# Memory keys turned by transposing DMAs in 16-bit halves, joined where a head's attention begins

## The chip, the cores and the metric

The kernel runs on one core of one Trainium2 chip. The metric is the device time of one execution in microseconds. The kernel is compared with itself after one change; the inputs and the result are the same.

## The reference

One decoder layer over 256 tokens of width 2048, in fp32: half a SwiGLU block, a mixer of two head groups, cross-attention over 256 memory rows, half a SwiGLU block, and a final norm. The change touches only the keys of the cross-attention:

```python
def cross_attention(hn, memn, w_q, w_kv, w_o):
    q = (hn @ w_q).reshape(b, s, X_HEADS, X_HEAD_DIM)      # 4 heads of 512
    kv = memn @ w_kv
    k = kv[..., :D_MODEL].reshape(b, m, X_HEADS, X_HEAD_DIM)
    v = kv[..., D_MODEL:].reshape(b, m, X_HEADS, X_HEAD_DIM)
    scores = jnp.einsum('bshd,bmhd->bhsm', q, k) * (X_HEAD_DIM ** -0.5)
    probs = jax.nn.softmax(scores, axis=-1)
    out = jnp.einsum('bhsm,bmhd->bshd', probs, v).reshape(b, s, D_MODEL)
    return out @ w_o
```

A score sums over the 512 features of a head, so queries and keys must both lie with features on the partitions, while the projection leaves them with tokens (or memory rows) on the partitions. Somebody has to turn them.

## The kernel before

Every fp32 operand of a large product is split into two parts, hi (a cast on ACT, line 147) and lo (a subtraction on DVE, line 148), and a product is three matmuls: hi by hi, lo by hi, hi by lo. All large matmuls are issued in line 411; their tiles are named after the unit (mk0, mk1, wo, xq, xo) with P, Q or R behind. A unit multiplies eight chunks of 256 input features by two blocks of 512 output columns for both token blocks of 128. Some chunks ("S" in the lists of kinds) use seven block products in place of eight, with sums of the weight blocks formed on DVE (tiles ending in t, lines 320 to 324). Weights come by one 1 MB load a chunk from SP's queue (lines 318 and 341) into three raw buffers, and are split into two pairs of buffers.

The order of TensorE's instructions is that of the program, pinned by hand. The other engines' orders, SP's DMA issues among them, are made by a list scheduler that goes by the program's order and by when operands and buffers are ready in its model; on the chip each engine then runs its own list in order. While a chunk is multiplied, `side_step` runs after every six matmuls and takes one piece of other work from the list `side`: generators that yield the number of steps to wait. `later` holds functions that are called after a number of chunks (0: with the chunk whose end put them there). Buffers come from rotating pools: `s2` (six of 128x512 fp32), `m4` (twelve of 128x1024), and four PSUM banks for everything that isn't an accumulator (`bank`).

The units stand in this order: mk0 and mk1 (keys of heads 0 and 1, then 2 and 3), wo (two halves of the mixer's output), xq (queries of heads 0 and 1, then 2 and 3), xo (two halves). A key unit leaves, for each head, two tiles of 128 memory rows by 512 features (`kr`, tile name mk). Before the change `memory_keys` turns them in two pieces of side work a head: four TensorE transposes (line 1248) into a PSUM bank, and one DVE copy (line 1249) into the m4 tile mkT. At the head's attention, `attend_memory` first turns and splits the queries (xqTp, xqT, line 1286), then splits the whole of mkT with one cast and one subtraction of 1024 columns (`split4`, tile mkh, which names both parts), waits four steps of side work, and multiplies queries by keys (xs, line 152).

The feed-forward blocks already turn their activations by DMA (`rows_done` and `joined`, lines 657 to 679). ACT separates the two 16-bit halves of each fp32 word (f1w), a transposing DMA on SP turns both halves of 128 columns at a time (f1a), and ACT interleaves the halves again when the tile is needed (f1r).

Of the kernel before, what the change touches and what calls it, by code (L numbers as in the profile page):

```python
# [10 lines left out]
U16 = mybir.dt.uint16  # L11
# [4 lines left out]
P = 128  # L16
T = 256
TB = 2
# [15 lines left out]
def layer_kernel(  # L34
# [22 lines left out]
    nc = tc.nc  # L57
# [13 lines left out]
    def nm(s):  # L71
        uid[0] += 1
        return f"{s}_{uid[0]}"

    def m4(s):
        return mid.tile([P, 1024], F32, tag="m4", name=nm(s))

    def s2(s):
        return tmp.tile([P, 512], F32, tag="s2", name=nm(s))

    def bank(s):
        return trp.tile([P, 512], F32, tag="tr", name=nm(s))
# [18 lines left out]
    ident = const.tile([P, P], F32, name="ident")  # L101
# [17 lines left out]
    h = const.tile([P, TB, D], F32, name="h")  # L119
# [26 lines left out]
    def split(hi, lo, src):  # L146
        nc.scalar.copy(hi, src)  # L147
        nc.vector.tensor_tensor(lo, src, hi.bitcast(F32), ALU.subtract)  # L148

    def products(o, passes):  # L150
        for i, (a, b) in enumerate(passes):
            nc.tensor.matmul(o, a, b, start=i == 0, stop=i == len(passes) - 1)
# [70 lines left out]
    def laid(kind, k, tb):  # L223
        return BASE[kind].index(f"A{tb + 1}{k + 1}")
# [199 lines left out]
    def side_add(gen):  # L424
        side.append([now[0], gen])

    def side_run(item):
        try:
            item[0] = now[0] + next(item[1])
        except StopIteration:  # L430
            side.remove(item)
# [16 lines left out]
    def until(done):  # L448

        while not done():  # L450
            side_run(side[0])

    def have(pairs, i):
        until(lambda: pairs[i] is not None)
        return pairs[i]
# [3 lines left out]
    later = []  # L459
# [192 lines left out]
    def ffn(s, get, rs, wgu, wd, on_block, first=None, on_token_block=None):  # L652
        acts = [None] * 22
        pairs = [None] * 22

        def rows_done(c, rows_):
            turned_ = m4(s + "a").bitcast(U16).rearrange("p (b c t) -> p b c t", b=TB, c=8)

            def turned(tb):
                w = s2(s + "w").bitcast(U16)  # L660
                nc.scalar.copy(
                    w.rearrange("p (h c) -> p h c", h=2),
                    rows_[tb].bitcast(U16).rearrange("p (c h) -> p h c", h=2),
                )
                nc.sync.dma_start_transpose(turned_[:, tb], w)
                for q in range(2):
                    acts[2 * c + q] = turned_

            for tb in range(TB):
                later.append((tb, lambda tb=tb: turned(tb)))  # L670

        def joined(i):
            turned_ = have(acts, i).rearrange("p b (h c) t -> p b c t h", h=2)
            raw = s2(s + "r")
            words = raw.bitcast(U16).rearrange("p (i t h) -> p i t h", i=4, h=2)
            q = 2 * (i % 2)
            for tb in range(TB):
                j, k = laid(KINDS_D[i], 0, tb), laid(KINDS_D[i], 1, tb)
                nc.scalar.copy(words[:, j:k + 1:k - j], turned_[:, tb, q:q + 2])
            return raw.rearrange("p (i t) -> p i t", i=4)  # L680
# [12 lines left out]
        def inner(i):  # L693
            if pairs[i] is None:
                raw = joined(i)
                pairs[i] = Pair(s + "a", KINDS_D[i])
                fill(s + "a", pairs[i], raw)
# [59 lines left out]
        for n, idx in enumerate(turns):  # L757
            half = n % 2
# [468 lines left out]
    def m4r(s):  # L1227
        return mid.tile([P, 1024], F32R, tag="m4", name=nm(s))

    def split4(s, src):  # L1230

        hi, lo = m4r(s), m4r(s)
        split(hi, lo, src)
        return hi, lo

    mk = [None] * 4

    def memory_keys(hd, rows_):

        flat = m4("mkT")  # L1240
        dst = flat.rearrange("p (k t) -> p k t", k=4)
        for half in range(2):
            yield 2 if half else 4
            pv = bank("mkTp").rearrange("p (k t) -> p k t", k=2)
            for i in range(2):
                for tb in range(TB):
                    c = (2 * half + i) * P
                    nc.tensor.transpose(pv[:, i, tb * P:(tb + 1) * P], rows_[tb][:, c:c + P], ident)
            nc.vector.tensor_copy(dst[:, 2 * half:2 * half + 2, :], pv)
        mk[hd] = flat  # L1250

    def key_rows(cb):
        kr = [[s2("mk") for _ in range(TB)] for _ in range(2)]

        def late(ps=None):
            if ps is not None:
                for name, tb, j in BLOCKS:
                    nc.scalar.copy(kr[j][tb], ps[tb, j])
            for j in range(2):
                side_add(memory_keys(2 * cb + j, kr[j]))  # L1260

        return kr, late

    for cb in range(2):
        kr, late_mk = key_rows(cb)
# [12 lines left out]
    def attend_memory(hd, rows_):  # L1278
        qh, ql = [m4r("xqT").rearrange("p (k t) -> p k t", k=4) for _ in range(2)]
        for half in range(2):  # L1280
            yield 1 if half == 0 else 1
            pv = bank("xqTp").rearrange("p (k t) -> p k t", k=2)
            for i in range(2):
                for tb in range(TB):
                    c = (2 * half + i) * P
                    nc.tensor.transpose(pv[:, i, tb * P:(tb + 1) * P], rows_[tb][:, c:c + P], ident)
            split(qh[:, 2 * half:2 * half + 2, :], ql[:, 2 * half:2 * half + 2, :], pv)
        until(lambda: mk[hd] is not None)
        kh, kl = [t.rearrange("p (k m) -> p k m", k=4) for t in split4("mkh", mk[hd])]
        yield 4  # L1290
        ps = bank("xs")
        pv = ps.rearrange("p (b m) -> p b m", b=2)
        for tb in range(TB):
            passes = [(q[:, k, tb * P:(tb + 1) * P], m[:, k, :])
                      for k in range(4) for q, m in ((qh, kh), (qh, kl), (ql, kh))]
            products(pv[:, tb, :], passes)
        mx = tiny.tile([P, TB], F32, tag="xmx", name=nm("xmx"))
        nc.vector.tensor_reduce(out=mx, in_=pv, axis=AX.X, op=ALU.max)
        nc.vector.tensor_scalar_mul(mx, mx, -XS)
        pr = s2("pr").rearrange("p (b m) -> p b m", b=2)  # L1300
        den = tiny.tile([P, TB], F32, tag="xden", name=nm("xden"))
        for tb in range(TB):
            nc.scalar.activation(
                pr[:, tb, :], pv[:, tb, :], AF.Exp, bias=mx[:, tb:tb + 1], scale=XS,
                accum_out=den[:, tb:tb + 1],
            )
        nc.vector.reciprocal(den, den)
        for tb in range(TB):
            nc.vector.tensor_scalar_mul(pr[:, tb, :], pr[:, tb, :], den[:, tb:tb + 1])
        vh, vl = [t.rearrange("p (b c) -> p b c", b=2) for t in split4("mvh", mv[hd])]  # L1310
        yield 5
        ptv = bank("xpT").rearrange("p (b t) -> p b t", b=2)
        for b in range(2):
            for tb in range(TB):
                nc.tensor.transpose(
                    ptv[:, b, tb * P:(tb + 1) * P], pr[:, tb, b * P:(b + 1) * P], ident
                )
        ph, pl = [
            tmp.tile([P, 512], F32R, tag="s2", name=nm("xpTs")).rearrange("p (b t) -> p b t", b=2)
            for _ in range(2)  # L1320
        ]
        split(ph, pl, ptv)
        yield 3
        for half in range(2):
            pv = bank("xo").rearrange("p (k t) -> p k t", k=2)
            for i in range(2):
                dt_ = 2 * half + i
                passes = [(m[:, b, dt_ * P:(dt_ + 1) * P], p[:, b, :])
                          for b in range(2) for m, p in ((vh, ph), (vh, pl), (vl, ph))]
                products(pv[:, i, :], passes)  # L1330
            i = 2 * hd + half
            kind = KINDS_O[i]
            p = Pair("xo", kind)
            if kind == "N":
                split(p.base[0].rearrange("p k t -> p (k t)"),
                      p.base[1].rearrange("p k t -> p (k t)"),
                      pv.rearrange("p k t -> p (k t)"))
            else:
                raw = s2("xor").rearrange("p (k t) -> p k t", k=4)
                for k in range(2):  # L1340
                    for tb in range(TB):
                        nc.scalar.copy(raw[:, laid(kind, k, tb), :], pv[:, k, tb * P:(tb + 1) * P])
                fill("xo", p, raw)
            xo[i] = p
            yield 1
# [147 lines left out]
```

## Time and profile before

| | us |
|---|---|
| median of three runs | 2039.45 |
| lowest and highest | 2039.23 and 2040.15 |
| the profiled execution | 2038.53 |
| its span | 2036.8 |

| engine | busy us |
|---|---|
| TensorE (PE) | 2019.8 |
| weight loads (PEld) | 1671.6 |
| DVE | 1858.2 |
| ACT | 1297.9 |
| POOL | 36.3 |

The rows of the profile name an engine, a line, an operation and the tiles, written as out<-in. The span is what the profile covers; the time beside it is the execution's own. A matmul's busy time overlaps with that of its neighbours, since the engine takes the next before the last has ended, so its cost in a full queue is read from the distance of starts. In brackets behind a row stand the idle time of the engine before it and what ended that.

### The profile page before, as it was taken

Reading aid. Unit: us, or ns where it says so; the run is one execution under the profiler, and the core shown is the slowest. Engines: PE = TensorE matmul, PEld = TensorE weight load, DVE = VectorE, ACT = ScalarE, POOL = GpSimd, SP = SyncE. Lnnn points to the kernel's source line nnn. Section 1 sums busy time; section 2 is a strip of 40 time slices with the busy share of each in tenths; the row PEclk is TensorE's granted clock in tenths of the full one; section 3 lists DMA queues with packets and bytes.
Section 4 is the critical chain, followed back from the end, with each engine's and each line's share of the span. In section 5 each row is a group of like instructions: output and inputs, shape, how many; then the busy total and the mean of one; then the engine's idle time right before and its main releaser. Section 6 shows DMA issues by size and latency. Waiting matters only on the chain.

```text
span 2036.8 us, 24300 instructions
## 1 busy us (share of the span) xinstructions
PE 2019.8 (99%) x9235; PEld 1671.6 (82%) x9235; DVE 1858.2 (91%) x1998; ACT 1297.9 (64%) x1432; POOL 36.3 (2%) x57
## 2 busy tenths in 40 slices
PE   9999999999999999999999999999999999999998
PEld 8788888888888888888888888888888888888886
DVE  6999999999999978988988987899999999999998
ACT  7865656567665766655556655675656666676664
POOL 0000000000000010100000000000000000000000
PEclk9999999999999999999999999999999999999999
DMA  8666666666555565545555544556566656665563
GB/s 312 195 209 232 214 219 197 232 217 218 204 192 205 187 243 176 196 166 183 193 182 179 198 161 145 186 186 218 199 234 210 217 213 225 220 215 209 186 225 127
DMA packets 106884, 413.72 MB, mean 203 GB/s; under 512 B 53376, under 2 KB 55440, under 8 KB 59664
## 3 DMA queue, kind: packets, MB, share of 16 engines
q1 hardware_dynamic: 104320, 405.04, 57.5%
q0 software_dynamic: 2016, 6.30, 0.9%
q8 instruction: 72, 1.18, 0.2%
q10 hardware_dynamic: 432, 0.84, 0.1%
q14 instruction: 44, 0.36, 0.1%
HBM read 398.52 MB, written 2.10 MB: 197 GB/s over the span
## 4 chain that ended last, share of the span: by engine, by line
PE 85%; DVE 8%; issue 3%; ACT 1%; DMA 1%; SPq 0%; POOL 0%; POOLq 0%; DVEq 0%; ACTq 0%
PE f2gQ L411 13%; PE f1gQ L411 12%; PE f2dQ L411 6%; PE f1dQ L411 6%; PE f1gP L411 5%; PE f2gP L411 4%; PE xqQ L411 3%; PE f2dP L411 3%; PE f1dP L411 3%; PE woQ L411 2%; PE xoQ L411 2%; PE f2dR L411 2%; PE f1dR L411 2%; DVE f1gwl L148 2%; PE vQ L411 2%
## 5 line engine op out<-in xcount | busy, mean ns | idle before, releaser
L148 DVE TENSOR_TENSOR f1gwl<-f1gw,f1gwh 128x1536 fp32r<-128x1536 f32 (+2 forms) x94 | 181.6, 1934 | 23.3 <-ACT f1gwh L147 22.4
L147 ACT CAST f2gwh<-f2gw 128x1536 fp32r<-128x1536 f32 (+1 forms) x88 | 150.3, 1711 | 59.6 <-PE f2gQ L411 39.2
L148 DVE TENSOR_TENSOR f2gwl<-f2gw,f2gwh 128x1536 fp32r<-128x1536 f32 (+1 forms) x88 | 179.2, 2037 | 9.6 <-ACT f2gwh L147 9.6
L147 ACT CAST f1gwh<-f1gw 128x1536 fp32r<-128x1536 f32 (+2 forms) x94 | 153.0, 1629 | 44.4 <-PE f1gQ L411 18.0
L147 ACT CAST f1gth<-f1gt 128x1024 fp32r<-128x1024 f32 x76 | 79.9, 1051 | 102.7 <-DVE f1gt L320 67.7
L147 ACT CAST f2gth<-f2gt 128x1024 fp32r<-128x1024 f32 x82 | 85.9, 1049 | 69.7 <-DVE f2gt L324 40.4
L411 PE MATMUL f2gQ<-f2gwh,n4fh 128*128 128x512 f32 x317 | 124.2, 392 | 1.5 <-DVE f2gv L570 1.5
L411 PE MATMUL f2gQ<-f2gwh,n4fl 128*128 128x512 f32 x317 | 123.4, 389 | 0.0
L411 PE MATMUL f1gQ<-f1gwh,n1fl 128*128 128x512 f32 x286 | 111.4, 390 | 1.7 <-DVE n1fl L148 1.7
L411 PE MATMUL f1gQ<-f1gwh,n1fh 128*128 128x512 f32 x286 | 111.6, 390 | 0.0
L147 ACT CAST f2dwh<-f2dw 128x2048 fp32r<-128x2048 f32 (+1 forms) x44 | 77.4, 1759 | 47.5 <-PE f2dQ L411 39.5
L147 ACT CAST f1dwh<-f1dw 128x2048 fp32r<-128x2048 f32 (+1 forms) x44 | 77.3, 1757 | 43.7 <-PE f1dQ L411 42.7
L148 DVE TENSOR_TENSOR f1dwl<-f1dw,f1dwh 128x2048 fp32r<-128x2048 f32 (+1 forms) x44 | 92.0, 2091 | 11.3 <-ACT f1dwh L147 11.2
L148 DVE TENSOR_TENSOR f2dwl<-f2dw,f2dwh 128x2048 fp32r<-128x2048 f32 (+1 forms) x44 | 92.1, 2092 | 11.2 <-ACT f2dwh L147 11.1
L148 DVE TENSOR_TENSOR f2gtl<-f2gt,f2gth 128x1024 fp32r<-128x1024 f32 x82 | 99.7, 1219 | 1.0
L411 PE MATMUL f2gQ<-f2gwl,n4fh 128*128 128x512 f32 x317 | 96.7, 389 | 0.0
L148 DVE TENSOR_TENSOR f1gtl<-f1gt,f1gth 128x1024 fp32r<-128x1024 f32 x76 | 92.2, 1217 | 0.5
L411 PE MATMUL f1gQ<-f1gwl,n1fh 128*128 128x512 f32 x286 | 86.9, 389 | 0.0
L411 PEld LDWEIGHTS f2gQ<-f2gwh,n4fh 128*128 128x128 f32 x317 | 59.5, 188 | 15.9 <-DVE f2gv L570 3.7
L411 PEld LDWEIGHTS f2gQ<-f2gwl,n4fh 128*128 128x128 f32 x317 | 59.4, 188 | 12.3
L411 PEld LDWEIGHTS f2gQ<-f2gwh,n4fl 128*128 128x128 f32 x317 | 59.5, 188 | 12.1
L411 PE MATMUL f2gP<-f2gwh,n4fh 128*128 128x512 f32 x176 | 68.6, 390 | 0.0
(823 smaller groups left out, 6057.8 us busy)
## 6 DMA issues: line engine op xcount, KB each, us to landing
f2gw<-in_w_gu SPq DMA_DIRECT2D x88, 1024.0 KB, 5.1
f1gw<-in_w_gu SPq DMA_DIRECT2D x86, 1024.0 KB, 4.9
f1dw<-in_w_down SPq DMA_DIRECT2D x44, 1024.0 KB, 4.8
f2dw<-in_w_down SPq DMA_DIRECT2D x44, 1024.0 KB, 4.8
wow<-in_w_out SPq DMA_DIRECT2D x16, 1024.0 KB, 4.8
xqw<-in_w_xq SPq DMA_DIRECT2D x16, 1024.0 KB, 4.8
xow<-in_w_xo SPq DMA_DIRECT2D x16, 1024.0 KB, 4.8
qw<-in_w_in SPq DMA_DIRECT2D x8, 1024.0 KB, 4.8
```

What stands on the lines that cost most here:

```text
L147: nc.scalar.copy(hi, src)
L148: nc.vector.tensor_tensor(lo, src, hi.bitcast(F32), ALU.subtract)
L411: nc.tensor.matmul(self.banks[name], x, y, start=name not in self.begun, stop=self.left[name] == 0)
```

## The change

The two pieces of side work that turned the keys of a head are gone, with their transposes, banks and copies. In their place stands, called through `later`, the helper `turned_rows`, taken out of the feed-forward block: for each head and block of memory rows one ACT copy into an s2 tile (mkw) and one transposing DMA from SP's queue. The first head of a unit is turned with the chunk that ends the unit, the second one chunk later. `mk[hd]` now holds the turned halves. `keys_split`, called where `split4` was, joins them: for each half of the features two ACT copies into an s2 tile (mkr), then a cast and a subtraction of 512 columns into mkh and mkl. The feed-forward block calls the same helpers with its work unchanged.

```diff
+    def turned_rows(s, dst, src):
+        w = s2(s + "w").bitcast(U16)
+        nc.scalar.copy(
+            w.rearrange("p (h c) -> p h c", h=2), src.bitcast(U16).rearrange("p (c h) -> p h c", h=2)
+        )
+        nc.sync.dma_start_transpose(dst, w)
+
+    def tile_turned(s):
+        return m4(s).bitcast(U16).rearrange("p (b c t) -> p b c t", b=TB, c=8)
+
+    def by_block(turned):
+        return turned.rearrange("p b (h c) t -> p b c t h", h=2)
+
+    def words_of(raw, n):
+        return raw.bitcast(U16).rearrange("p (i t h) -> p i t h", i=n, h=2)
...
     def memory_keys(hd, rows_):
-        flat = m4("mkT")
-        dst = flat.rearrange("p (k t) -> p k t", k=4)
+        mk[hd] = tile_turned("mkT")
+        for tb in range(TB):
+            turned_rows("mk", mk[hd][:, tb], rows_[tb])
+
+    def keys_split(hd):
+        hi, lo = m4r("mkh"), m4r("mkl")
+        turned_ = by_block(mk[hd])
         for half in range(2):
-            yield 2 if half else 4
-            pv = bank("mkTp").rearrange("p (k t) -> p k t", k=2)
-            for i in range(2):
-                for tb in range(TB):
-                    c = (2 * half + i) * P
-                    nc.tensor.transpose(pv[:, i, tb * P:(tb + 1) * P], rows_[tb][:, c:c + P], ident)
-            nc.vector.tensor_copy(dst[:, 2 * half:2 * half + 2, :], pv)
-        mk[hd] = flat
+            raw = s2("mkr")
+            for tb in range(TB):
+                nc.scalar.copy(
+                    words_of(raw, 4)[:, tb::2], turned_[:, tb, 2 * half:2 * half + 2]
+                )
+            cols = slice(half * 512, (half + 1) * 512)
+            split(hi[:, cols], lo[:, cols], raw)
+        return hi, lo
...
             for j in range(2):
-                side_add(memory_keys(2 * cb + j, kr[j]))
+                later.append((j, lambda j=j: memory_keys(2 * cb + j, kr[j])))
...
-        until(lambda: mk[hd] is not None)
-        kh, kl = [t.rearrange("p (k m) -> p k m", k=4) for t in split4("mkh", mk[hd])]
+        kh, kl = [t.rearrange("p (k m) -> p k m", k=4) for t in keys_split(hd)]
```

More of the change, by code (lines that the diff above doesn't have):

```diff
@@ L656, in rows_done @@
         def rows_done(c, rows_):
-            turned_ = m4(s + "a").bitcast(U16).rearrange("p (b c t) -> p b c t", b=TB, c=8)
+            t = tile_turned(s + "a")
             def turned(tb):
[L660 to L665, printed above, removed]
+                turned_rows(s, t[:, tb], rows_[tb])
                 for q in range(2):
-                    acts[2 * c + q] = turned_
+                    acts[2 * c + q] = t
             for tb in range(TB):
@@ L672, in joined @@
         def joined(i):
-            turned_ = have(acts, i).rearrange("p b (h c) t -> p b c t h", h=2)
+            turned_ = by_block(have(acts, i))
             raw = s2(s + "r")
-            words = raw.bitcast(U16).rearrange("p (i t h) -> p i t h", i=4, h=2)
+            words = words_of(raw, 4)
             q = 2 * (i % 2)
```

## The prediction

> **What bounds the kernel now.** I read the engine totals first, then the stretches around the change, then the rows of the tiles it touches.
>
> ```profile
> PE 2019.8 (99%) x9235; PEld 1671.6 (82%) x9235; DVE 1858.2 (91%) x1998; ACT 1297.9 (64%) x1432; POOL 36.3 (2%) x57
> ```
>
> ```profile
> 1000.00:1020.00 20.00, 20.00 (x98) 16.55 (x97) 19.71 (x21) 11.78 (x11) 0.00 (x0) 1.00 0.52 187
> 1040.00:1060.00 20.00, 20.00 (x100) 16.52 (x99) 15.76 (x19) 7.71 (x7) 0.00 (x0) 1.00 0.51 180
> 1180.00:1200.00 20.00, 19.64 (x106) 16.53 (x105) 16.97 (x19) 14.72 (x16) 0.00 (x0) 1.00 0.46 159
> ```
>
> The first fence is the engines' totals, the second three stretches of 20 us, whose columns are length, then PE, weight load, DVE, ACT and POOL busy, granted clock, DMA share and GB/s. The keys are produced in the first two stretches and used from the third on. TensorE is full in all of them at a clock of 1.00, but for 0.36 us in the third; ACT has 5 to 12 us of every 20 free, DVE 0.3 to 4. So an instruction taken from TensorE is worth what it takes of its queue, as long as nothing new arrives late.
>
> That worth is not the duration that the tile's rows show.
>
> ```profile
> L1248 PE MATMUL mkTp<-ident,mk x32: 270/272/273, 1008.7 to 1071.3; 128*128 128x128 f32 x32
> L1249 DVE COPY mkT<-mkTp x8: 678/682/693, 1009.3 to 1071.7; 128x512 f32<-128x512 f32 x8
> ```
>
> ```profile
> 1008.25 0.39 PE L411 MATMUL mk1Q<-mk1wh,mTfh 128*128 128x512 f32 x1
> 1008.47 0.39 PE L411 MATMUL mk1Q<-mk1wh,mTfl 128*128 128x512 f32 x1
> 1008.70 0.60 PE L1248 MATMUL mkTp<-ident,mk 128*128 128x128 f32 x4
> 1009.06 0.48 PE L411 MATMUL mk1Q<-mk1wh,mTfh 128*128 128x512 f32 x1
> 1009.37 0.39 PE L411 MATMUL mk1Q<-mk1wh,mTfl 128*128 128x512 f32 x1
> ```
>
> Instructions overlap on this engine: two neighbouring matmuls of 512 columns start 0.22 to 0.23 us apart (1008.25, 1008.47), though each lasts 0.39. From the last start before the four transposes (1008.47) to the second after them (1009.37) 0.90 us pass, where two regular steps take 0.45. A group of four costs 0.45 us, 0.11 each.
>
> **The change, step by step.**
>
> *Removed from TensorE and DVE.* Four heads by two halves by four transposes are 32 transposes in 8 groups: 8 x 0.45 = 3.6 us, on a queue that is full at each of them, so this goes off the end. The 8 copies out of PSUM (8 x 0.682 = 5.5 us of DVE) go too. I give them nothing: TensorE waited for none of them. The eight banks and eight pieces of side work go as well; the pieces behind them in the side list (those of ya and yb) come up to a step earlier, which on a full TensorE is an exchange of order.
>
> *Added: turning.* For each head and token block one ACT copy that separates the 16-bit halves, and one transposing DMA on SP. The same pair stands in the first feed-forward block.
>
> ```profile
> L661 ACT COPY f1w<-f1gp x10: 1029/1036/1047, 101.8 to 472.9; 128x1024 uint16<-128x1024 uint16 x10
> L665 SPq DMA_TRANSPOSE f1a<-f1w x22: 1237/1275/1687, 52.0 to 478.1; - x22
> ...
> DMA to landing us min/median/max: 3.0/3.2/5.7
> ```
>
> The last line is the time from issue to landing. So 8 x 1.04 = 8.3 us of ACT and 8 x 1.28 = 10.2 us of SP's queue, landing after 3.2 us. The rows are complete at 1003.4 and 1048.1, and the keys are first read at 1188.
>
> ```profile
> L572 DVE TENSOR_TENSOR mk<-mk0Q,mk0z x1: 681/681/681, 1002.7 to 1002.7; 128x512 f32<-128x512 f32 x1
> L572 DVE TENSOR_TENSOR mk<-mk1Q,mk1z x1: 680/680/680, 1047.4 to 1047.4; 128x512 f32<-128x512 f32 x1
> L147 ACT CAST mkh<-mkT x4: 1047/1048/1054, 1188.2 to 1249.9; 128x1024 fp32r<-128x1024 f32 x4
> L148 DVE TENSOR_TENSOR mkh<-mkT,mkh x4: 1215/1217/1226, 1189.6 to 1251.0; 128x1024 fp32r<-128x1024 f32 x4
> ```
>
> The cover of the turning is some 140 us long, so its latency costs nothing. What it can cost is a place in ACT's and SP's order. ACT has room at the end of a key unit (6.25 us before 1001.87):
>
> ```profile
> 1001.87 1.92 ACT L147 CAST mk1wh<-mk1w 128x2048 fp32r<-128x2048 f32 x1 [6.25 <-PE mk0Q L411]
> 1012.14 1.91 ACT L147 CAST mk1wh<-mk1w 128x2048 fp32r<-128x2048 f32 x1 [0.50 <-PE mk1Q L411]
> 1006.23 0.33 SPq L318 DMA_DIRECT2D mk1w<-in_w_xkv  x1
> ```
>
> ```profile
> 1019.60 0.93 PE mk1P L411 x4
> ```
>
> ```profile
> mk1w<-in_w_xkv SPq DMA_DIRECT2D x8, 1024.0 KB, 4.9
> ```
>
> On SP a transpose waits at the head for its copy, and the weight load behind it waits too. The load of 1006.23 has 1 MB and lands after 4.9 us by its group's row, so at 1011.1; its cast began at 1012.14 and ended at 1014.05, and TensorE takes that weight at 1019.60. The load may slip 1.0 + 5.5 = 6.5 us before TensorE waits. Two transposes in a row hold SP 2.6 us. POOL's queue gets nothing. Cost: 0, with an end at what a longer hold gives (rival below).
>
> *Moved: joining and splitting.* One cast and one subtraction of 1024 columns become, per head, four joining copies, two casts and two subtractions of 512.
>
> ```profile
> L679 ACT COPY f1r<-f1a x44: 665/679/695, 433.3 to 629.1; 128x512 uint16<-128x512 uint16 x44
> L147 ACT CAST f1afh<-f1r x22: 611/616/632, 437.6 to 631.2; 128x512 fp32r<-128x512 f32 x22
> L148 DVE TENSOR_TENSOR f1afl<-f1r,f1afh x22: 678/682/686, 438.7 to 633.7; 128x512 fp32r<-128x512 f32 x22
> ```
>
> That is ACT 4 x 0.68 + 2 x 0.62 - 1.05 = +2.9 us a head and DVE 2 x 0.68 - 1.22 = +0.15. They are in the way only if the products of queries and keys come to TensorE's head before the split is done:
>
> ```profile
> 1189.57 1.22 DVE L148 TENSOR_TENSOR mkh<-mkT,mkh 128x1024 fp32r<-128x1024 f32 x1
> 1193.96 3.02 PE L152 MATMUL xs<-mkh,xqT 128*128 128x256 f32 x24
> 1196.90 1.05 ACT L147 CAST mkh<-mkT 128x1024 fp32r<-128x1024 f32 x1 [1.72 <-PE xs L152]
> 1198.11 1.22 DVE L148 TENSOR_TENSOR mkh<-mkT,mkh 128x1024 fp32r<-128x1024 f32 x1
> 1200.92 3.04 PE L152 MATMUL xs<-mkh,xqT 128*128 128x256 f32 x24
> 1244.53 1.22 DVE L148 TENSOR_TENSOR mkh<-mkT,mkh 128x1024 fp32r<-128x1024 f32 x1
> 1250.62 3.02 PE L152 MATMUL xs<-mkh,xqT 128*128 128x256 f32 x24
> ```
>
> Head 0: the split ends at 1190.79, the products begin at 1193.96, so 3.2 us are spare against 2.9 + 0.15 = 3.1 wanted; besides, the second half of the keys is wanted some 0.7 us after the products begin. Head 1: 1199.33 against 1200.92, 1.6 spare. But here ACT waited 1.72 us for a buffer that the products of head 0 set free (a cast needs one of the twelve m4 buffers); the joining copies need only s2 buffers and keys that have lain there for over 100 us, so they can run in that wait, and then 1.2 us of the 2.9 are left. Head 2: 1245.75 against 1250.62, 4.9 spare. Four joins and two casts can also be cut by a weight cast of 1.91. Ends: 0 and, for head 0, 1.9 us, for head 1 the uncovered 2.9 + 0.15 - 1.6 = 1.5, together 3.4. I take 0, as three of the four numbers (3.2, 4.9, and 1.6 + 1.72 of wait) cover it.
>
> A bound below nothing: the one stall of this stretch, TensorE waiting for the last query row.
>
> ```profile
> 1185.33 0.33 PE L1286 MATMUL xqTp<-ident,xqz 128*128 128x128 f32 x1 [0.36 <-ACT xqz L1351]
> ```
>
> ACT's order there is made anew with the joins in it, so 0.4 may go, or grow by a join or two (0.6 each). Taken: no change. The same holds for the second feed-forward block, whose order is also made anew and which is not full everywhere; the waits of its commonest matmul sum to 1.5 us, so I allow 1 us either way.
>
> ```profile
> L411 PE MATMUL f2gQ<-f2gwh,n4fh 128*128 128x512 f32 x317 | 124.2, 392 | 1.5 <-DVE f2gv L570 1.5
> ```
>
> *Sum.* -3.6 + 0 + 0 + 0. The profiled execution took 2038.53 us around a span of 2036.8, which becomes 2034.9; it lies 0.9 below the median of the runs, 2039.45, which becomes 2035.9. That is -0.18%, just inside 0.2% (4.1 us), about what a measurement of this kernel can tell from no change.
>
> **Rivals.**
>
> *More than the sum:* the 3.6 us and one or two of the small stalls with them, 4.1 to 6 us, so 2033.5 to 2035.3. For it: DVE is relieved by 5.5 + 4 x 1.22 - 8 x 0.68 = 4.9 us in a stretch where it was busy 19.71 of 20, and it ends the waits in the second feed-forward block. Against it: in the stretches of the change TensorE waited once, for ACT.
>
> *Each transpose is worth its duration:* 32 x 0.272 = 8.7 us, so 2030.7. For it: the row of the tile. Against it: the starts at 1008.47 and 1009.37. The Trainium skill ("TensorE: Matmul & The Clock Gate", Part 4) gives about 275 ns for a transpose in a kernel; by that figure the gain would be an estimated 8.8 us. The trace agrees with it as a duration (272 ns) and not as a cost in a full queue (0.11 us).
>
> *The heads wait for their keys:* part or all of 3.4 us is given back, so 2036.5 to 2039.3. For it: 3.1 wanted of 3.2 spare at head 0, and ACT busy 14.72 of 20 there before 5.8 us more come. Against it: the wait of 1.72 at head 1 and the idle ACT ahead of the query rows, in which joins can run.
>
> *Slower: SP's queue.* If a transpose is put on SP ahead of a load long before its copy can run, the load slips. It decides from 6.5 us of slip on. A hold as long as the longest wait that SP shows in this stretch, 9.6 us, costs 9.6 - 6.5 = 3.1 us of TensorE; there are four such places (two heads after each of two units), so up to 12.4 - 3.6 = +8.8 us, 2048.3, and with two of them 2042.0.
>
> ```profile
> SPq L341 <- DVE xqwl L148: 61.4, 10, 9.6
> ```
>
> ```profile
> 102.81 2.62 SPq L665 DMA_TRANSPOSE f1a<-f1w  x2
> 105.52 0.53 SPq L318 DMA_DIRECT2D f1gw<-in_w_gu  x1
> ```
>
> Against it: in the feed-forward block two transposes and the load behind them run through in 2.7 us. The Trainium skill ("VectorE: DVE Perf Modes", Rules for kernel authors) advises TensorE for a 128x128 transpose whenever PSUM will do as the target, which speaks against this change. [...]
>
> **How the numbers follow.** The forecast, 2035.4 to 2036.5: 0.41. More than the sum: 0.26. Durations: 0.05. Heads wait: 0.15. SP's queue: 0.13, of which 0.03 within 0.2%. Faster by over 0.2% takes the second and third, 0.31; within 0.2% the forecast, the heads and 0.03, 0.59; slower 0.10. The range 2033.5 to 2039.5 holds the forecast, the stalls both ways and the heads, 0.82; the likeliest case alone has 2035.4 to 2036.5.
>
> **What would show it.** Right: no mkTp rows; 32 fewer TensorE instructions, and the first product of the head 0 scores some 3.6 us earlier; TensorE at 20.00 in the stretches above; transposes of mk landing within some 6 us, and weight casts not waiting for loads longer than before. Wrong: idle time on TensorE or its weight load ahead of the scores (xs), released by ACT or DVE for mkh; an idle wait before wowh or mk1wh products; a weight load that starts late behind a transpose; or a head 0 that starts 8 us earlier.

## The result, and the profile after

The changed kernel takes 2033.45 us (median of eight runs, 2032.99 to 2035.32) against 2039.34 (eight runs, 2037.55 to 2040.94): ratio 0.9975, interval 0.9965 to 0.9984, so 5.9 us less by the medians. The profiled execution took 2033.63 us with a span of 2031.9, 4.9 less than the span before.

The engines' totals on the page of the changed kernel, then the stretches shown of the kernel before (the same columns):

```profile
PE 2015.5 (99%) x9203; PEld 1668.8 (82%) x9203; DVE 1853.6 (91%) x1994; ACT 1313.2 (65%) x1460; POOL 34.4 (2%) x57
```

```profile
1000.00:1020.00 20.00, 20.00 (x94) 16.54 (x93) 17.46 (x20) 14.81 (x15) 0.00 (x0) 1.00 0.78 215
1040.00:1060.00 20.00, 20.00 (x93) 16.54 (x92) 14.64 (x16) 11.29 (x11) 0.00 (x0) 1.00 0.78 204
1180.00:1200.00 20.00, 19.99 (x118) 17.20 (x117) 18.10 (x20) 17.50 (x26) 0.00 (x0) 1.00 0.31 109
```

32 matmuls fewer, DVE 4.6 us less, ACT 15.3 more, and TensorE still full, now in the third stretch too. The rows of the new work, by tile:

```profile
L153 ACT COPY mkw<-mk x8: 1037/1042/1046, 1004.5 to 1053.2; 128x1024 uint16<-128x1024 uint16 x8
L156 SPq DMA_TRANSPOSE mkT<-mkw x8: 1237/1316/4127, 1005.5 to 1054.2; - x8
DMA to landing us min/median/max: 3.2/5.3/6.6
```

```profile
L1263 ACT COPY mkr<-mkT x16: 658/684/712, 1173.7 to 1248.7; 128x512 uint16<-128x512 uint16 x16
L147 ACT CAST mkh<-mkr x8: 616/622/632, 1184.9 to 1251.1; 128x512 fp32r<-128x512 f32 x8
L148 DVE TENSOR_TENSOR mkl<-mkr,mkh x8: 680/684/693, 1186.1 to 1251.7; 128x512 fp32r<-128x512 f32 x8
```

To see where the time went, I cut the span twice: at the first mk0Q matmul of the key unit mk0 (2.2 us behind the unit's first matmul, in both kernels), and at the last matmul ahead of a wait that both kernels have in xo (for n4r). Of the timelines of TensorE, first the kernel before, then the changed one:

```profile
961.65 0.48 PE L411 MATMUL mk0Q<-mk0wh,mTfh 128*128 128x512 f32 x1
1317.46 0.39 PE L411 MATMUL xoQ<-xoth,xofl 128*128 128x512 f32 x1
```

```profile
962.43 0.48 PE L428 MATMUL mk0Q<-mk0wh,mTfh 128*128 128x512 f32 x1
1314.16 0.39 PE L428 MATMUL xoQ<-xoth,xofl 128*128 128x512 f32 x1
```

The part ahead of the change was 0.78 us longer in this execution. The stretch of the change took 351.73 in place of 355.81: 4.08 us less. The rest (the end of xo and the second feed-forward block) took 2031.9 - 1314.16 = 717.74 in place of 719.34: 1.60 us less, although no instruction of the second feed-forward block is changed, and the list of each engine (TensorE, DVE, ACT and SP) has the same order there as before.

### The profile page after: what moved, and what is told of

Same layout as the page of the kernel before. It is cut to its first block, busy times and chain, and to the rows that moved or that the text cites. A ratio compares the mean times of both kernels' runs of the same rounds, so it can differ in the third digit from the quotient of the medians.

```text
span 2031.9 us, 24271 instructions
## 1 busy us (share of the span) xinstructions
PE 2015.5 (99%) x9203; PEld 1668.8 (82%) x9203; DVE 1853.6 (91%) x1994; ACT 1313.2 (65%) x1460; POOL 34.4 (2%) x57
## 4 chain that ended last, share of the span: by engine, by line
PE 85%; DVE 9%; issue 3%; ACT 2%; DMA 2%; SPq 0%; POOL 0%; POOLq 0%; DVEq 0%; ACTq 0%
PE f1gQ L428 12%; PE f2gQ L428 12%; PE f2dQ L428 6%; PE f1dQ L428 6%; PE f1gP L428 5%; PE f2gP L428 4%; PE xqQ L428 3%; PE f2dP L428 3%; PE f1dP L428 3%; PE woQ L428 2%; PE xoQ L428 2%; PE f2dR L428 2%; PE f1dR L428 2%; DVE f1gwl L148 2%; PE vQ L428 2%
```

## The experiments

So there were two things to explain: whether the 4.1 us in the stretch are TensorE's queue (queue theory) or the relief of DVE (DVE theory), and where the 1.6 us behind it come from. Every run was profiled, and its span cut in the same two places; `stretch` and `rest` are from its one trace, the ratio from all its runs. A trace is one execution, and not always a typical one: that of act_copies took 2036.50 us where its runs have a median of 2038.12, that of ya 2033.31 against 2035.00.

| kernel | transposes of keys or pads on TensorE | ratio to before (interval) | stretch us | rest us |
|---|---|---|---|---|
| before | 32 | 1 | 355.81 | 719.34 |
| same_before | 32 | 1.0006 (0.9997 to 1.0015) | 355.83 | 719.95 |
| act_copies | 32 | 0.9999 (0.9990 to 1.0008) | 355.46 | 717.55 |
| before96 | 128 | 1.0047 (1.0035 to 1.0060) | 365.98 | 718.99 |
| changed | 0 | 0.9975 (0.9965 to 0.9984) | 351.73 | 717.74 |
| same_after | 0 | 0.9975 (0.9966 to 0.9985) | 351.74 | 718.17 |
| half | 16 | 0.9987 (0.9979 to 0.9996) | 353.57 | 717.91 |
| pad32 | 32 | 1.0002 (0.9993 to 1.0011) | 355.52 | 721.49 |
| pad112 | 112 | 1.0046 (1.0034 to 1.0058) | 364.13 | 719.87 |
| pad128 | 128 | 1.0047 (1.0033 to 1.0060) | 366.01 | 718.71 |
| pad160 | 160 | 1.0075 (1.0061 to 1.0089) | 369.51 | 719.80 |
| q01 | 0, and 16 of the queries gone | 0.9997 (0.9988 to 1.0006) | 353.45 | 722.30 |
| ya | 0, and 16 of ya gone | 0.9979 (0.9970 to 0.9988) | 350.30 | 719.59 |
| yab | 0, and 32 of ya and yb gone | 0.9987 (0.9978 to 0.9996) | 353.27 | 720.35 |

### Both kernels once more

> The kernel before once more, unchanged, for what a comparison with itself shows and for a second trace. Every theory: ratio 1.000. If the waits for f2gv in the second feed-forward block (1.5 us in the first trace) and the time of the first feed-forward block (the key unit began at 961.65 there and at 962.43 in the changed kernel) differ here by some tenths too, those differences are from one execution to the next and not the change's.

> The changed kernel once more. Every theory: ratio 0.9975 (interval of the first comparison 0.9965 to 0.9984), 5 us below before. Queue theory (the gain is what 32 transposes take of TensorE's queue, and the wait for the last query row): from the first matmul of the key unit to the last of the second xo unit 4.1 us less than before, the rest of the difference not in the stretch of the change.

The stretch came out again to 0.02 us in each kernel. In these four traces the part ahead varies by 0.8 us, and the rest of one kernel by 0.4 to 0.6, so a difference of 1 us in the rest needs more than one trace.

### Transposes put back: 32 and 128

```diff
+    def padding():
+        for half in range(2):
+            yield 2 if half else 4
+            pv = bank("pad")
+            for i in range(4):                      # 16 in pad128
+                nc.tensor.transpose(pv[:, (i % 4) * P:(i % 4 + 1) * P], ident, ident)
...
                 later.append((j, lambda j=j: memory_keys(2 * cb + j, kr[j])))
+                side_add(padding())
```

> The changed kernel with 32 transposes of the identity put back as side work in the places where the 32 key transposes were, into a PSUM bank that nobody reads; keys are turned by DMA as in the changed kernel. Queue theory: 3.6 us of the gain are gone, some 2035.5 if the changed kernel has 2032, ratio to before 0.9985 to 0.9995. DVE theory (the gain comes from the eight copies that DVE no longer makes): nothing is lost, ratio 0.9975. Duration theory (each transpose is worth its 0.27 us): 8.7 us are lost, ratio 1.0015 or more.

> As pad32, with four times as many transposes of the identity (16 in each of the eight places). Queue theory: 128 x 0.11 = 14 us above the changed kernel, ratio to before 1.0045. Duration theory: 128 x 0.272 = 35 us above it, ratio 1.0145. DVE theory: as the changed kernel until TensorE's extra work shows, so no forecast below queue theory's.

The stretch bears out the queue theory, to within 0.3 us: 32 pads cost 3.78 us, 128 cost 14.28, so 0.118 and 0.112 each. By tile, the row of pad128 still shows the duration:

```profile
L1262 PE MATMUL pad<-ident x128: 270/273/273, 1008.4 to 1081.5; 128*128 128x128 f32 x128
```

But the whole of pad32 lost 6.2 us against same_after on the same chip (2040.21 and 2034.02), not 3.6, and the 96 further pads of pad128 then cost 8.5, less than the 10.5 that the stretch shows for them. What was too much in the first step and too little in the second lies in the rest: 721.49 and 718.71.

### The copies on ACT

```diff
-            nc.vector.tensor_copy(dst[:, 2 * half:2 * half + 2, :], pv)
+            nc.scalar.copy(dst[:, 2 * half:2 * half + 2, :], pv)
```

> The kernel before, with the eight copies of turned keys out of PSUM made by ACT in place of DVE; the 32 transposes stay on TensorE. DVE is relieved by 5.5 us as in the change, TensorE is not. Queue theory: ratio 1.000 (0.9995 to 1.0005). DVE theory: ratio 0.9975 to 0.9985.

Ratio 0.9999 (0.9990 to 1.0008), where the DVE theory has 0.9985 or less. DVE was busy 1853.8 us, as little as in the changed kernel, and the stretch kept 355.46 of its 355.82 us. The DVE theory is out. The 0.36 us that did go are the wait for the last query row (xqz), which is absent here with all transposes in place. It is absent in before96 and pad32 as well, and back in ya (0.36) and yab (0.38), so it is not tied to the transposes, nor to DVE's relief; what makes it come and go stays open.

### What happened behind the stretch

The second feed-forward block turns its activations by pairs of transposing DMAs on SP, with a weight load behind each pair. Around the eighth pair the DMA list of the kernel before (same_before, from the pair's issue on) and that of same_after differ. Of each queue the list has packets, MB and share of the DMA engines' time:

```profile
q1 hardware_dynamic: 1644, 0.41, 64.1%
q8 instruction: 1, 0.02, 1.9%
issues: line engine op xcount, KB each, median us to landing
f2gw<-in_w_gu SPq DMA_DIRECT2D x1, 1024.0 KB, 7.8
f2a<-f2w SPq DMA_TRANSPOSE x2, 3.9
```

```profile
q1 hardware_dynamic: 1698, 0.43, 66.2%
issues: line engine op xcount, KB each, median us to landing
f2gw<-in_w_gu SPq DMA_DIRECT2D x1, 1024.0 KB, 5.3
f2a<-f2w SPq DMA_TRANSPOSE x2, 3.2
```

In the first, one packet of the instruction queue q8 falls among the transposes. Their median is 3.9 in place of 3.2 us: the first still lands after 3.22, the second after 4.58 in place of 3.14. The load behind them lands after 7.8 in place of 5.3. The GB/s by fortieths of the 8 us from that load on show the hole (same_before):

```profile
GB/s 207 211 207 278 210 131 12 0 6 9 10 9 693 0 614 0 614 369 287 614 0 614 614 0 614 615 41 614 655 41 614 451 205 655 164 492 655 41 615 655
```

For some 1.2 us hardly anything moves. ACT's next cast then waits for the load, in same_before and in same_after:

```profile
1689.58 1.48 ACT L147 CAST f2gwh<-f2gw 128x1536 fp32r<-128x1536 f32 x1 [4.25 <-DMA f2gw<-in_w_gu]
```

```profile
1683.20 1.49 ACT L147 CAST f2gwh<-f2gw 128x1536 fp32r<-128x1536 f32 x1 [1.79 <-DMA f2gw<-in_w_gu]
```

DVE is busy 77.7 to 78.6 of every 80 us from 1400 to 1640 in same_before, so it cannot make good 2.5 us at once, and TensorE waits for it; the waits of TensorE in the second block (total us, times, longest), pad32 first, then the changed kernel:

```profile
PE f2gQ L428 <- DVE f2gv L587: 1.7, 3, 0.9
PE f2gP L428 <- DVE f2gwl L148: 1.4, 2, 1.1
```

```profile
PE f2gQ L428 <- DVE f2gv L587: 0.6, 2, 0.3
PE f2gP L428 <- DVE f2gwl L148: 0.3, 1, 0.3
```

Whose instructions are these? The page of the kernel before has for the whole span:

```profile
q8 instruction: 72, 1.18, 0.2%
```

That is 16.4 KB to a packet, and TensorE ran 2 x 9235 instructions: 256.5 to a packet. In the four runs with 9315 matmuls or more (pad112, pad128, pad160, before96) it had 73. So the packets fit TensorE's stream in blocks of 256, or 128 matmuls with their weight loads. If that is what they are, the change shifted that stream by 64 instructions against the transposes of the second block, and a shift by 128 matmuls should undo itself (fetch theory). The Trainium skill ("Runtime: NRT & Kernel Launch", Instruction fetch mechanics) has the same blocks of 256 instructions in 16 KiB, and calls the cost of crossing one mostly hidden. The block agrees with the counts here; the cost was not hidden for those packets that delayed transposing DMAs and the load behind them (up to 2.6 us of TensorE, below).

### The shift tried: 96 more before the change, 160, and 112

```diff
             pv = bank("mkTp").rearrange("p (k t) -> p k t", k=2)
+            for i in range(12):
+                nc.tensor.transpose(pv[:, i % 2, :P], ident, ident)
             for i in range(2):
```

> The kernel before, with 12 transposes of the identity ahead of each group of four key transposes, in the same bank and overwritten by them: 96 more transposes, so 128 in these places. Queue theory for the stretch from the first matmul of the key unit to the last of the second xo unit: 96 x 0.1115 = 10.7 us more than before, 366.5. Fetch theory for the rest (the second feed-forward block gains 1.5 us because TensorE's stream of instructions is shorter and one of its fetches no longer falls on a pair of transposing DMAs; 128 matmul pairs are one block): 128 transposes put the stream where the changed kernel has it, so no instruction packet in the pair of transposes near 1690 and a second block of 717.7 to 718.7 us after the last matmul of xo, against 719.3 and 720.0 before; ratio 1.0045. Against it, relief theory (the second block is shorter because DVE or the order of work is relieved ahead of it): 719.3 to 720.0, ratio 1.0053.

> The changed kernel with 160 transposes of the identity in the eight places (20 each). Stretch of the change: 351.7 + 160 x 0.1115 = 369.6 us in both theories. Fetch theory: 160 is 32 beyond a block of 128, so the second feed-forward block has the alignment of the kernel before and of pad32: an instruction packet in the pair of transposes near 1695, the load behind it landing after 6 to 8 us, and 719.3 to 721.5 us after the last matmul of xo. Relief theory: as pad128 and the changed kernel, 717.7 to 718.7.

> The changed kernel with 112 transposes of the identity in the eight places (14 each). Stretch of the change: 351.7 + 112 x 0.1115 = 364.2 us. 112 is 16 short of a block of 128, the alignment of q01, whose keys and queries are ordered otherwise. Fetch theory: instruction packets in the third and the eighth... of the pairs of transposes where q01 had them (the fourth at 1512 and the ninth at 1719 there, so near 1525 and 1732 here), loads behind them landing after 6 to 8 us, and a second block of 720 to 722 us; ratio to before some 1.0050, although pad128 with 16 transposes more had 1.0047. Without it (q01's second block was long because of its own order): 717.7 to 719, ratio 1.0035.

The place of the packet came out as forecast in each run (for pad112 the pairs meant are the fourth and the ninth, as the parenthesis of its expectation has them). The first ten pairs of the second block, numbered in order, where a packet of q8 began 2.6 to 4.0 us after the pair's issue, with the median landing of the two transposes and the landing of the load behind them:

| kernel | transposes modulo 128 | pair, its landing, the load's landing (us) | rest |
|---|---|---|---|
| before, same_before, act_copies | 32 | eighth: 4.1, 3.9, 4.0; load 6.0, 7.8, 5.8 | 719.3, 720.0, 717.6 |
| pad32, pad160 | 32 | eighth: 4.0, 3.9; load 7.8, 7.4 | 721.5, 719.8 |
| changed, same_after, pad128, before96 | 0 | none | 717.7, 718.2, 718.7, 719.0 |
| q01, ya, pad112 | 112 | fourth: 3.8 each; load 7.9, 5.6, 7.8; ninth: 3.9, 4.0, 3.8; load 8.2, 8.0, 7.5 | 722.3, 719.6, 719.9 |
| yab | 96 | second: 4.9; load 6.6 | 720.4 |
| half | 16 | first: 4.0; load 5.8 | 717.9 |

Of these 140 pairs in 14 traces, the second transpose landed after 4.4 to 4.9 us in all 13 of the table and after 3.1 to 3.3 in the other 127. A packet that began within half a microsecond of the pair's issue delayed nothing (0.10 us after it in the first pair of before: 3.1 and 3.2 us; 0.43 after it in the sixth of half: 3.3 and 3.1). Nor did a packet of the other instruction queue, q14, that began 2.4 us after the issue (the ninth of half: 3.3 and 3.1). So it is not enough that a packet falls into a pair; when it begins, and on which queue, decides.

What a delayed pair costs is not fixed: where the load still landed after 5.8 us (act_copies, half) the rest was as short as without a packet; with a load of 6 to 8 us it was 719.3 to 722.3, against 717.7 to 719.0 in the four traces with none. On the size the forecasts were less good: pad112 had 719.87 where 720 to 722 was expected, and before96 and pad128 lie near the lower end of the other group (before96 0.3 us above its forecast).

The medians of all runs, not only one trace each, point the same way. A kernel's ratio times 2039.3 us, less its stretch, is the time outside the stretch by all its runs. Set against the kernel before, it is 0.6 to 1.0 us shorter for the four with 0 in the table, 0.2 to 1.6 longer for the other four with 32, and 1.1 to 1.8 longer for the three with 112. The interval of each ratio is some 2 to 3 us either way, so the groups show this and no single run does.

TensorE's matmuls behind the second cut are the same 3115 in the same order in every run, so one can be set against the other. Between those that start at 1692.27 and 1740.20 in the changed kernel, behind the eighth pair, the five traces with a packet in that pair took longer: before by 0.8 us, act_copies 0.6, pad160 2.2, same_before 2.5, pad32 2.6. Of the others, same_after, before96 and pad128 took 0.0 to 0.3 longer, and q01 and pad112 no longer than the changed kernel. But half took 0.4, yab 0.5 and ya 0.8 longer, also without a packet in that pair, so a loss under 1 us does not prove one.

This also divides the 1.6 us of the first comparison: 0.8 arose at the eighth pair and 0.9 near 1470, and what else differs is some tenths either way. Ahead of 1470 no instruction packet had delayed a pair. The load behind the second pair landed after 6.2 us in the kernel before and 5.2 in the changed one, ACT's cast waited for it (before, then changed), and TensorE waited for DVE 29 us later:

```profile
1441.56 1.48 ACT L147 CAST f2gwh<-f2gw 128x1536 fp32r<-128x1536 f32 x1 [2.60 <-DMA f2gw<-in_w_gu]
1470.38 0.50 PE L411 MATMUL f2gQ<-f2gwh,n4fh 128*128 128x512 f32 x1 [0.60 <-DVE f2gv L570]
```

```profile
1437.11 1.48 ACT L147 CAST f2gwh<-f2gw 128x1536 fp32r<-128x1536 f32 x1 [1.46 <-DMA f2gw<-in_w_gu]
```

In yab, whose second pair did have a packet and whose load took 6.6 us, TensorE lost 1.1 us at the same matmul; same_before, with a load of 5.0, lost nothing there. Why the load of the kernel before was late is open.

Nor is the packet gone from the changed kernel. The block has an eleventh pair, whose two transposes are issued 4.1 us apart with a load between them. In the four traces with 0 a packet began 0.8 to 2.0 us after the issue of the second one, which landed after 4.5 to 5.0 us (3.2 to 3.8 in the other ten), and the load after 6.4 to 7.0 (5.0 to 5.6). TensorE lost nothing by it: over the next 78 us all 14 traces keep step to 0.05 us. So what the change moved is the meeting, from a place where it costs to one where it does not.

### Half of the change

```diff
-                later.append((j, lambda j=j: memory_keys(2 * cb + j, kr[j])))
+                if cb:
+                    side_add(keys_on_pe(2 * cb + j, kr[j]))     # as before the change
+                else:
+                    later.append((j, lambda j=j: memory_keys(2 * cb + j, kr[j])))
```

> Half of the change: heads 0 and 1 have their keys turned by DMA, heads 2 and 3 by TensorE with the copies on DVE and one cast and one subtraction of 1024 columns. 16 transposes less than before. Queue theory: the stretch of the change 1.8 us shorter for the transposes, and 0.4 with it for the wait for the last query row of heads 0 and 1, so 353.6 to 354.0. Fetch theory has the alignment 16, which no run had yet: the second block is short (717.7 to 718.7) if no pair has a packet, else 719.3 to 722; ratio 0.9985 or 0.9995.

The stretch, 353.57, is 2.25 less than before: 16 x 0.117 = 1.9 and the 0.36 of the wait. The packet fell into the first pair and cost nothing that the rest shows. Ratio 0.9987, between the two expected.

### More of the same: queries of heads 0 and 1, and the mixer's output

In q01 the query rows of heads 0 and 1 go the way of the keys, with eight steps of side work ahead of the joins:

```diff
+        if hd < 2:
+            t = tile_turned("xqt")
+            yield 1
+            for tb in range(TB):
+                turned_rows("xq", t[:, tb], rows_[tb])
+            yield 8
...
+            for half in range(2):
+                raw = s2("xqr")
+                for tb in range(TB):
+                    nc.scalar.copy(
+                        words_of(raw, 4)[:, tb::2], turned_[:, tb, 2 * half:2 * half + 2]
+                    )
```

> The changed kernel with the query rows of heads 0 and 1 turned and joined in the same way (four ACT copies, four transposing DMAs, eight joins more; 16 transposes fewer on TensorE), with eight steps of side work between the DMA and the joins. Queue theory: 16 x 0.11 = 1.8 us below the changed kernel if the scores of these heads are moved late enough, ratio to before 0.9965; ACT was busy 17.5 of 20 us there and gets some 8 us more, so if the weight casts slip, TensorE waits and the gain is lost, ratio 0.9975 or more.

It lost everything. The stretch was 1.7 us longer than the changed kernel's, not 1.8 shorter: 3.5 us were given back. TensorE's waits in the stretch that the changed kernel does not have sum to 2.6 us, and the two largest are for ACT:

```profile
1203.91 0.51 PE L428 MATMUL xqP<-xqwh,n3fh 128*128 128x512 f32 x1 [0.87 <-ACT xqwh L147]
1209.15 0.39 PE L169 MATMUL xs<-mkh,xqT 128*128 128x256 f32 x1 [0.82 <-ACT pr L1336]
```

And its packets met two pairs of transposes in the rest, which is 4.6 us longer than the changed kernel's.

For ya and yab the rows of one or both halves of the mixer's output are turned once they are scaled, and joined pair by pair:

```diff
+        by_dma = k0 in (0,)                                    # (0, 4) in yab
+        if by_dma:
+            t = [tile_turned(s + "t") for _ in range(2)]
+            for half in range(2):
+                for tb in range(TB):
+                    turned_rows(s, t[half][:, tb], rows_[tb][:, half * 512:(half + 1) * 512])
...
+            if by_dma:
+                ny[k0 + i] = pair_joined(s, KINDS_O[k0 + i], by_block(t[i // 2]), 2 * (i % 2), gcol + 2 * i)
+                continue
```

> The changed kernel with the first half of the mixer's output (ya) turned and joined in the same way ahead of w_out: 16 transposes less on TensorE, 8 ACT copies, 8 transposing DMAs and 8 joins more in a stretch where ACT was busy 11 to 15 of 20 us. Queue theory: stretch of the change 1.8 us shorter, 349.9. Fetch theory: the alignment of pad112 and q01, so the second block is 720 to 722 us and the whole no faster than the changed kernel, ratio 0.9975 to 0.9985; without it 0.9965.

> As ya, with the second half (yb) too: 32 transposes less than the changed kernel, 64 less than before. Queue theory: stretch of the change 3.6 us shorter, 348.1, if the weight casts of w_out do not slip behind the new copies. Fetch theory: an alignment that no run had yet, so the second block may be short or long; ratio 0.9955 if short, 0.9970 if long. Against both: yb is ready late (its transposes began at 1061 before), and the ACT copies and a landing of 5 us come ahead of its pairs, so that TensorE may wait 2 to 5 us for them, ratio 0.997 or more.

In ya the stretch gave 1.43 of the 1.8 us (the wait for xqz, 0.36, is back), and the rest, with two packets, is 1.4 to 1.9 us longer: 0.9979, where the changed kernel has 0.9975, so no gain that the intervals show. In yab the late rows are waited for, as its counter-theory had it, and so is a weight's lo part (why it is late no run separates):

```profile
1066.80 0.50 PE L448 MATMUL woP<-wowh,ybfl 128*128 128x512 f32 x1 [1.04 <-DVE ybfl L142]
1086.31 0.50 PE L448 MATMUL woP<-wowl,ybfh 128*128 128x512 f32 x1 [1.41 <-DVE wowl L148]
```

No version tried shows a gain over the changed kernel.

## Why the prediction was right or wrong

*What a transpose is worth:* right. 0.112 to 0.118 us each by the pads against 0.11 from the starts around one group; 3.8 us for the 32. The rival of 0.272 us each is out, though the duration in the rows stayed 0.273.

*DVE's copies at nothing:* right (act_copies).

*Turning hidden:* right in the end, with a term mis-sized and a spare misread. I took 3.2 us from issue to landing and 2.6 us of SP for two transposes, though the row shown has a longest of 5.7. The eight landed after 5.3 (median), at most 6.6, and SP's rows show the second pair of mk0 taking 5.4:

```profile
1005.54 2.63 SPq L156 DMA_TRANSPOSE mkT<-mkw  x2
1008.26 0.53 SPq L335 DMA_DIRECT2D mk1w<-in_w_xkv  x1
1008.90 5.42 SPq L156 DMA_TRANSPOSE mkT<-mkw  x2
1014.41 0.53 SPq L358 DMA_DIRECT2D mk1w<-in_w_xkv  x1
```

The two copies for that pair had ended by 1008.36, so SP was not waiting for them: the last issue itself took 4.13 us. The load that went at 1006.23 before goes at 1008.26 and lands 3.4 us later, at 1014.46 (2.6 once the 0.78 of this execution is taken off); that of 1011.72 goes at 1014.41, 1.9 us later. So loads did slip, as the slower rival has it, but by another mechanism than its transpose waiting for a copy. The 6.5 us of spare were no measure of it: the cast at 1012.14 is not of the load of 1006.23. That load is the fifth of mk1w, the fifth cast is the one at 1016.27, and in the changed kernel the cast at 1012.41 begins before the load has landed. Its first reader is DVE, at 1012.07, so only 1.0 us was spare there, and in the changed kernel DVE does wait for it:

```profile
1014.55 1.23 DVE L337 TENSOR_TENSOR mk1t<-mk1w 128x1024 f32<-128x1024 f32 x1 [0.35 <-DMA mk1w<-in_w_xkv]
```

TensorE takes that weight at 1025.38 before and at 1025.22 after, and waits for nothing in the key units. How long a hold it would have taken to reach it was not tried.

*Heads 0 and 1 in time:* right. In the changed kernel's timelines the split of head 0 ends at 1187.34 and its products begin at 1190.58; for head 1 it is 1195.90 and 1197.54. Both spares are those of before (3.2 and 1.6).

```profile
1181.80 1.24 ACT L1263 COPY mkr<-mkT 128x512 uint16<-128x512 uint16 x2
1186.06 1.28 DVE L148 TENSOR_TENSOR mkl<-mkr,mkh 128x512 fp32r<-128x512 f32 x2
1190.58 0.28 PE L169 MATMUL xs<-mkh,xqT 128*128 128x256 f32 x1
1194.61 1.29 DVE L148 TENSOR_TENSOR mkl<-mkr,mkh 128x512 fp32r<-128x512 f32 x2
1197.54 0.28 PE L169 MATMUL xs<-mkh,xqT 128*128 128x256 f32 x1
```

The four joins of head 0 ran from 1173.70 on, two of them ahead of the last query row, in the idle ACT that the prediction named against the rival that the heads wait; its sum had counted on such cover for head 1 alone.

*The small stalls at no change:* this is the step that failed. The wait for xqz went (0.36), and the rest became 1.6 us shorter in the first two traces and 1.8 in the repeats, beyond the 1 us allowed. So the time fell where "more than the sum" has it, 0.05 us below its far end of 2033.5, with 2035.9 as the likeliest. That was luck: the reason given there was DVE's relief, and act_copies, with the same relief and no gain, shows it to be wrong. What the runs show in its place is that TensorE's stream is 64 instructions shorter, and that no block of it arrives among the transposes of the eighth pair any more; one meets the eleventh, where it costs nothing. That the place of the packet came out as forecast in four runs (none at the eighth pair in before96, the eighth pair in pad160, the fourth and the ninth in pad112 and ya) carries that. That this packet is the whole of the 1.6 us is not shown, and in the first comparison it is not: 0.8 us arose at the eighth pair. Its cost there varied from 0.6 to 2.6 us between traces of the same alignment.

## What to carry to other kernels

On an engine that is full, price an instruction by the distance of the starts around it and check it by padding: 32 transposes moved off TensorE gave 3.8 us, under half of the 8.7 us that their durations add up to. Moving work to another engine was free here where that engine had idle time and the results were wanted much later: the keys, wanted some 140 us later, cost TensorE nothing on an ACT with 5 to 12 of every 20 us free. The queries, wanted some 10 us later on an ACT busy 17.5 of 20, cost 3.5 us; which of the two did it was not separated. And a change of well under 1% can owe a quarter of its gain to a part of the kernel that it does not touch; cut the span at fixed matmuls before crediting the edit with all of it, and compare matmul by matmul before crediting one cause with the remainder.

## What the runs showed of the hardware that was not expected

- A packet of the instruction queue that began 2.6 to 4.0 us after the issue of a pair of transposing DMAs delayed the second of them from 3.1 to 3.3 us to between 4.4 and 4.9, in all 13 such pairs of the second block; one that began within 0.5 us of the issue did not. The DMA engines were then almost idle for about 1.2 us (same_before), and the load behind the pair landed after 5.6 to 8.2 us, where the other loads behind pairs took 4.9 to 6.2.
- In the changed kernel two pairs of transposing DMAs, issued 3.4 us apart with a load between them, landed after 3.2 and 6.4 us (medians), and the second pair held SP for 5.4 us in place of 2.6. In half, with no instruction packet near, they landed after 3.2 and 6.2.
